# Modulation rows and bias pieces in a fused two-block kernel: where the pieces stand between the rows

## The chip, the core and the metric

The kernel runs on one core of a Trainium2 chip. PE (TensorE) multiplies, DVE (VectorE) and ACT (ScalarE) work on rows of 128 lanes, POOL (GpSimd) does small elementwise work and issues its own DMAs, SP only issues DMAs. Each engine takes its instructions in program order: one that waits holds up all behind it. The metric is the time of one execution on the device in microseconds; lower is better.

## The reference, cut to what matters

Two transformer blocks run one after the other on 256 tokens of width 1024. What the change touches lies in the second block: its modulation vector and the biases of its 32 experts.

```python
cs = jax.nn.silu(c.astype(jnp.float32))
mod = cs @ w_ada[l] + b_ada[l]                       # 6 x 1024 values
sh_a, sc_a, gt_a, sh_f, sc_f, gt_f = jnp.split(mod, 6, axis=-1)
h = modulate(rms_norm(x, g_mix[l]), sh_a, sc_a)
...
def expert_block(args):
    xb, e = args
    u = xb @ w1[e] + b1[e]
    ...
    return a @ w2[e] + b2[e]
```

The modulation needs only c, and the biases need nothing else, so both can be prepared at any time before the second block uses them.

## The kernel before, in words

**The dense stage.** The first 880 us or so are a list of 128 matrix products (`plan`): `w_in`, `w_br_sb`, `w_gate` with `w_br_df`, `w_out`, the feed-forward products and then those of the second block. SP loads each product's weights in tiles `w` of 1 MB. `feed_halves` splits every half tile into a rounded high part on ACT (line 106) and the rest on DVE (line 107); the two are called `hl`, and PE multiplies with them in three products per tile (lines 213 to 215). The pool of `hl` has three buffers, so at most two halves lie ready while PE works through a third. One half is 24 products of 256 columns.

**Ticks.** `run_w` calls `tick()` after every 12 products. A tick lets side work (generators in `sides`) put its next instructions into the program; a generator's `yield n` asks for its next turn n ticks later. Everything is fixed when the program is built: a tick is a place in the instruction streams, no time.

**The side work `ada`.** It computes `mod` in 48 rows of 128 values. `row(j)` has POOL issue a DMA of 512 KB into one of two buffers `wa` (line 267); one custom DVE instruction multiplies the row with `cs` and sums it (line 280). In the 19th round and the five after it, `ada` also calls `bias_parts` once (lines 994 to 1001): POOL loads a piece of the experts' biases into one of the same two buffers `wa` (there called `b`), does six small conversions on it and writes the result to DRAM as `bias_parts`. A row for which there is no free buffer waits, on POOL's queue, until the piece has been written. The rows pause while `st["hold"]` is set, during the last down products of the first block's feed-forward part. `drain_names` (used by `close_heads`) runs ticks with no product between them until the attention heads are done.

**The expert stage**, the rest of the time, streams 402 MB of expert weights through SP's queue.

Of the kernel before, what the change touches and what calls it, by code (L numbers as in the profile page):

```python
# [34 lines left out]
]  # L35


LAG = dict(rs=2, ad0=1, lam=4, bq=12, el=4, bp=18, r1=52, wo=3, rg=21, ada=7, head=6, ffn=2, n2=3, n2b=6, sb0=4, sb1=6, vt=3, df0=1, df1=4, df2=3, df3=8, df4=4, rt0=6, rt1=6, dl0=2, dl1=4, dl2=11, dl3=1)
LAG["in"] = 4


@with_exitstack
def tile_two_blocks(ctx, tc, A, out, dbg=None):
# [31 lines left out]
    def pair(name, n=S, wide=False):  # L75
        return bigt(name + "h", n, F32R, wide=wide), bigt(name + "l", n, F32R, wide=wide)
# [110 lines left out]
    def side(gen, lag=1):  # L187
        sides.append([state["tick"] + lag, gen])
# [62 lines left out]
    def ada():  # L251

        more = bias_parts()
        cs = tmp.tile([P, D], F32, tag="cs", name="cs", bufs=1)
        nc.gpsimd.dma_start(cs, A["c2"].to_broadcast([P, D]))
        t = tmp.tile([P, D], F32, tag="wa", name="wa", bufs=2)
        yield 3
        act(t, cs, AF.Exp, scale=-1.0)
        nc.gpsimd.tensor_scalar_add(t, t, 1.0)
        yield 3  # L260
        for r in range(0, D, 256):
            nc.vector.reciprocal(t[:, r:r + 256], t[:, r:r + 256])
            yield 1
        nc.gpsimd.tensor_mul(cs, cs, t)
        def row(j):
            t = tmp.tile([P, D], F32, tag="wa", name="wa", bufs=2)
            nc.gpsimd.dma_start(t, A["w_ada_2"][j])
            return t

        rows = [row(0)]  # L270
        for j in range(48):
            if j >= LAG["bp"]:
                next(more, 0)
            if j < 47:
                rows.append(row(j + 1))
            yield LAG["ada"]
            while st.get("hold"):
                yield 2
            t = rows.pop(0)
            nc.vector.tensor_tensor_reduce(out=t, in0=t, in1=cs, scale=1.0, scalar=vec[:, V_BADA + j:V_BADA + j + 1],  # L280
                                           op0=ALU.mult, op1=ALU.add, accum_out=mod[:, j:j + 1])


    lam_init = 0.8 - 0.6 * math.exp(-0.3 * 0)
# [43 lines left out]
    def norm_in():  # L328
# [19 lines left out]
        nc.gpsimd.tensor_add(a[:, 0], a[:, 0], a[:, 1])  # L348
        side(in_factor(a), LAG["in"])
        st["os"] = pair("os")  # L350
        st["od"] = pair("od")

    def in_factor(a):
        ss = att.tile([P, 512], F32, tag="at", name="ss")
        mm(ss[:, :L], ones, a[:, 0], start=True, stop=True)
        rs = rsin
        v, t = small(L, "rs")
        first, rest = rsqrt_steps(rs, ss[:, :L], (v, t), 1.0 / D, eps, EPS)
        first()
        yield LAG["rs"]  # L360
        rest()
        st["rsin"] = rs
        st["rs"] = rs[:, NM:L].unsqueeze(1).to_broadcast([P, 2, S])
        st["late"]()
        side(ada(), LAG["ad0"])
        yield LAG["lam"]
        lam()
        yield 1
# [618 lines left out]
    def bias_parts():  # L987

        nc.gpsimd.dma_start(sel, A["sel"])
        for c in range(6):  # L990
            c_ = slice(c * 512, (c + 1) * 512)
            br = tmp.tile([P, D], F32, tag="wa", name="b", bufs=2)
            b, r = br[:96, 0:512], br[:96, 512:768].bitcast(BF16)
            nc.gpsimd.dma_start(b, A["b12"][:, c_])
            nc.gpsimd.tensor_copy(r, b)
            nc.gpsimd.tensor_sub(b, b, r)
            nc.gpsimd.tensor_copy(r[32:64], b[32:64])
            nc.gpsimd.tensor_copy(r[64:96], b[64:96])
            nc.gpsimd.tensor_sub(b[64:96], b[64:96], r[64:96])
            nc.gpsimd.tensor_copy(r[64:96], b[64:96])  # L1000
            nc.gpsimd.dma_start(bsd.ap()[:, c_], r)
            yield

    def spread(to, cols):
        nc.gpsimd.tensor_mul(to, ident.unsqueeze(1).to_broadcast([P, 4, P]), cols.unsqueeze(2).to_broadcast([P, 4, P]))
# [598 lines left out]
```

## Time and profile before

| | |
|---|---|
| median of 3 runs | 1827.83 us (1824.49 to 1828.0) |
| the profiled execution, whole | 1826.24 us |
| its span in the profile | 1824.0 us |
| PE busy | 1739.4 us, 95% of the span |
| DVE busy | 875.0 us, 48% |
| ACT busy | 484.7 us, 27% |
| POOL busy | 123.9 us, 7% |
| mean DMA rate | 313 GB/s |

The span is the time from the first to the last instruction of the profiled execution; its own time is 2.2 us longer. Shares of busy time are means over two stages that have different limits, so they say little by themselves; the stretches below are what to read.

### The profile page before, as it was taken

How to read it: one execution, taken by the hardware profiler on the slowest of the kernel's cores; microseconds unless marked ns; L12 is line 12 of the kernel's file. 1: busy time of each engine (PE TensorE's matmuls, PEld its weight loads, DVE VectorE, ACT ScalarE, POOL GpSimd, SP SyncE). 2: the span in 40 equal slices, each digit the busy share in tenths (PEclk: the TensorE clock that was granted, in tenths of full speed). 3: DMA queues.
4: the chain of work that ended last, by engine and by line, in shares of the span. 5: the costliest groups of instructions: out<-in, count | busy, mean ns of one | idle time of the engine just before them, and what ended most of it. 6: DMA issues, size and time to landing. Idle time of an engine off the chain costs nothing. (4 is left out here: it accounts for less than half of the span.)

```text
span 1824.0 us, 25881 instructions
## 1 busy us (share of the span) xinstructions
PE 1739.4 (95%) x10942; PEld 1145.8 (63%) x10942; DVE 875.0 (48%) x1330; ACT 484.7 (27%) x754; POOL 123.9 (7%) x132
## 2 busy tenths in 40 slices
PE   8999998789999999999999999999999999999987
PEld 7999998789998999999733333333233323332322
DVE  7767776577778667776422223222222222222223
ACT  4545654244435644455300000000000000000001
POOL 2100004520003000000100000000000000000000
PEclk8999999799999999999999999999999999999999
DMA  6446455468665654566899999999999999999996
GB/s 220 170 167 229 158 193 186 167 209 341 245 216 179 245 179 168 204 223 226 309 416 424 423 425 424 424 422 424 422 425 424 423 424 423 424 423 425 422 425 261
DMA packets 107645, 571.82 MB, mean 313 GB/s; under 512 B 11022, under 2 KB 16070, under 8 KB 59654
## 3 DMA queue, kind: packets, MB, share of 16 engines
q1 hardware_dynamic: 96144, 538.46, 74.1%
q0 software_dynamic: 7904, 28.08, 4.6%
q10 hardware_dynamic: 3478, 3.59, 0.6%
q8 instruction: 87, 1.43, 0.3%
q14 instruction: 32, 0.26, 0.0%
HBM read 568.44 MB, written 4.02 MB: 314 GB/s over the span
## 5 line engine op out<-in xcount | busy, mean ns | idle before, releaser
L1265 PE MATMUL u<-mw,xe 128*64 128x512 f32 x2048 | 476.7, 600 | 18.1 <-DMA mw<-in_w_mlp_dram 17.3
L107 DVE TENSOR_TENSOR hl<-w,hl 128x1024 fp32r<-128x1024 f32 (+1 forms) x256 | 318.3, 1257 | 146.6 <-ACT hl L106 146.1
L1265 PEld LDWEIGHTS u<-mw,xe 128*64 128x64 f32 x2048 | 132.7, 136 | 300.1 <-issue 222.8
L106 ACT ACTIVATE hl<-w 128x1024 fp32r<-128x1024 f32 (+1 forms) x256 | 260.1, 1032 | 125.2 <-PE ps L215 74.7
L1299 PE MATMUL y<-mw,aT 128*64 128x512 f32 x992 | 227.7, 597 | 19.6 <-DMA mw<-in_w_mlp_dram 19.4
L1299 PEld LDWEIGHTS y<-mw,aT 128*64 128x64 f32 x992 | 67.2, 136 | 163.2 <-issue 102.0
L1319 DVE TENSOR_TENSOR macc<-macc,cp 128x512 f32<-128x512 f32 x124 | 79.7, 684 | 184.4 <-PE cp L1316 184.4
L213 PE MATMUL ps<-xnh,hl 128*128 128x256 f32 (+1 forms) x512 | 153.3, 299 | 2.4 <-ACT hl L106 2.4
L215 PE MATMUL ps<-xnh,hl 128*128 128x256 f32 (+1 forms) x512 | 149.2, 291 | 6.2 <-DVE hl L107 6.2
L214 PE MATMUL ps<-xnl,hl 128*128 128x256 f32 (+1 forms) x512 | 148.2, 289 | 0.0
L1285 ACT COPY aT<-ap 128x512 f32<-128x512 f32 x31 | 18.2, 586 | 425.6 <-PE ap L1283 425.6
L213 PE MATMUL ps<-h2h,hl 128*128 128x256 f32 x384 | 110.2, 287 | 0.0
L215 PE MATMUL ps<-h2h,hl 128*128 128x256 f32 x384 | 108.7, 283 | 0.0
L214 PE MATMUL ps<-h2l,hl 128*128 128x256 f32 x384 | 108.6, 283 | 0.0
L213 PEld LDWEIGHTS ps<-xnh,hl 128*128 128x128 f32 x512 | 99.2, 194 | 7.3 <-ACT hl L106 3.8
L215 PEld LDWEIGHTS ps<-xnh,hl 128*128 128x128 f32 x512 | 99.0, 193 | 7.3 <-DVE hl L107 7.3
L213 PE MATMUL ps<-hnh,hl 128*128 128x256 f32 x352 | 100.6, 286 | 0.0
L214 PE MATMUL ps<-hnl,hl 128*128 128x256 f32 x352 | 100.3, 285 | 0.0
L215 PE MATMUL ps<-hnh,hl 128*128 128x256 f32 x352 | 100.2, 285 | 0.0
L214 PEld LDWEIGHTS ps<-xnl,hl 128*128 128x128 f32 x512 | 99.0, 193 | 0.1
L1305 DVE TENSOR_TENSOR ys<-y,m 128x512 f32<-128x512 f32 x31 | 21.4, 692 | 138.4 <-PE y L1303 138.4
L1293 DVE COPY m<-gq 128x256 f32<-128x256 f32 x31 | 13.2, 425 | 144.1 <-PE gq L1291 144.1
(466 smaller groups left out, 2934.6 us busy)
## 6 DMA issues: line engine op xcount, KB each, us to landing
mw<-in_w_mlp_dram SPq DMA_DIRECT2D x383, 1024.0 KB, 19.7
w<-in_w_in_dram SPq DMA_DIRECT2D x60, 1024.0 KB, 4.9
wa<-in_w_ada_dram POOLq DMA_DIRECT2D x48, 512.0 KB, 4.8
w<-in_w_ffn_gate_dram SPq DMA_DIRECT2D x11, 1024.0 KB, 5.0
w<-in_w_ffn_up_dram SPq DMA_DIRECT2D x11, 1024.0 KB, 4.8
w<-in_w_gate_dram SPq DMA_DIRECT2D x8, 1024.0 KB, 5.4
w<-in_w_ffn_down_dram SPq DMA_DIRECT2D x8, 1024.0 KB, 5.4
w<-in_w_br_sb_dram SPq DMA_DIRECT2D x4, 1024.0 KB, 6.0
```

Of the source, the lines that this page charges most:

```text
L106: act(hi, src, AF.Copy)
L107: (eng or nc.vector).tensor_sub(lo, src, hi.bitcast(F32))
L213: mm(ps[m], hi[:, k, cs], xh[:, k0 + k, r], start=first, stop=False, skip_group_check=True)
L214: mm(ps[m], hi[:, k, cs], xl[:, k0 + k, r], start=False, stop=False, skip_group_check=True)
L215: mm(ps[m], lo[:, k, cs], xh[:, k0 + k, r], start=False, stop=last, skip_group_check=True)
L1265: mm(u[64 * hf:64 * hf + 64, c * 512:(c + 1) * 512], xk, wcol(hf, c), start=k == 0, stop=False)
L1285: nc.scalar.copy(aT, ap)
L1293: nc.vector.tensor_copy(gT, gq[:, :256])
L1299: mm(y[64 * hf:64 * hf + 64, :], a, wcol(hf), start=k == 0, stop=False)
L1305: nc.vector.tensor_mul(ys, y, gtf)
L1319: nc.vector.tensor_add(d, d, cp[hf])
```

## The change

The first two rows are asked for ahead of the loop. In each round the DVE instruction of the row now comes first; then, in six rounds, a piece of the biases, after which the generator rests for `LAG["bq"]`, 12 ticks; then the row after the next is asked for. The rest ahead of each DVE instruction is 6 ticks where it was 7. `bias_parts` yields `None` so that the loop can tell a piece from the end.

```diff
-LAG = dict(... bq=12, el=4, bp=18, ... ada=7, ...)
+LAG = dict(... bq=12, el=4, bp=18, ... ada=6, ...)
...
-        rows = [row(0)]
+        rows = [row(0), row(1)]
         for j in range(48):
-            if j >= LAG["bp"]:
-                next(more, 0)
-            if j < 47:
-                rows.append(row(j + 1))
             yield LAG["ada"]
             while st.get("hold"):
                 yield 2
             t = rows.pop(0)
             nc.vector.tensor_tensor_reduce(out=t, in0=t, in1=cs, ...)
+
+            if j >= LAG["bp"] and next(more, 1) is None:
+                yield LAG["bq"]
+            if j < 46:
+                rows.append(row(j + 2))
...
             nc.gpsimd.dma_start(bsd.ap()[:, c_], r)
-            yield
+            yield None
```

On every engine the other instructions keep their order; only the row's DVE instruction and POOL's row loads and pieces stand elsewhere between them. Three places follow.

DVE, from the products `w_gate` and `w_br_df` (`gt`, `m1l`) to the first of `w_out` (`xr`, `hnl`), before the change; `wa,mod<-wa,cs,c_vecs` is the instruction of a row:

```order
L107 TENSOR_TENSOR hl<-w,hl 128x1024
L280 ISA wa,mod<-wa,cs,c_vecs 128x1024
L280 ISA mod 128x1
L107 TENSOR_TENSOR hl<-w,hl 128x1024
L529 TENSOR_TENSOR gt<-ps,masks 128x512
L107 TENSOR_TENSOR hl<-w,hl 128x1024 x2
L280 ISA wa,mod<-wa,cs,c_vecs 128x1024
L280 ISA mod 128x1
L547 TENSOR_TENSOR gt<-gt,ysb 128x512
L548 TENSOR_TENSOR gt<-gt,ps 128x512
L549 TENSOR_TENSOR gt<-gt 128x512
L107 TENSOR_TENSOR m1l<-gt,m1h 128x512
```

The same place after the change:

```order
L107 TENSOR_TENSOR hl<-w,hl 128x1024 x2
L276 ISA wa,mod<-wa,cs,c_vecs 128x1024
L276 ISA mod 128x1
L530 TENSOR_TENSOR gt<-ps,masks 128x512
L107 TENSOR_TENSOR hl<-w,hl 128x1024 x2
L548 TENSOR_TENSOR gt<-gt,ysb 128x512
L549 TENSOR_TENSOR gt<-gt,ps 128x512
L550 TENSOR_TENSOR gt<-gt 128x512
L107 TENSOR_TENSOR m1l<-gt,m1h 128x512
L107 TENSOR_TENSOR hl<-w,hl 128x1024 x2
L582 TENSOR_TENSOR xr<-ps,xr 128x2x256
```

Before, a row comes after every three or four splits `hl`, in the rounds with a piece as well; now nine splits lie between two rows of such rounds.

POOL, from a piece to the next piece, reads the same before and after (here after, without the conversions between); what differs is which row the load in the middle brings: before it is the row that DVE's next such instruction takes, after it is the one after that.

```order
L1001 CAST b<-b 32x512
L1002 DMA bias_parts<-b 96x512
L267 DMA wa<-in_w_ada_dram 128x1024
L995 DMA b<-in_b_dram 96x512
L996 CAST b<-b 96x512
```

The load of the row moved to 12 ticks behind the piece in the order in which the program is written; on POOL alone that does not show.

DVE at the end of the heads, inside the ticks without products, before the change (`on` and `odl` are the last steps of a head):

```order
L529 TENSOR_TENSOR gt<-ps,masks 128x512
L280 ISA wa,mod<-wa,cs,c_vecs 128x1024
L280 ISA mod 128x1
L504 SCALAR_TENSOR_TENSOR on<-o,gsub,rsd 128x256
L107 TENSOR_TENSOR odl<-on,odh 128x256
L280 ISA wa,mod<-wa,cs,c_vecs 128x1024
L280 ISA mod 128x1
L504 SCALAR_TENSOR_TENSOR on<-o,gsub,rsd 128x256
L107 TENSOR_TENSOR odl<-on,odh 128x256
L107 TENSOR_TENSOR hl<-w,hl 128x1024 x2
```

The same place after the change:

```order
L530 TENSOR_TENSOR gt<-ps,masks 128x512
L276 ISA wa,mod<-wa,cs,c_vecs 128x1024
L276 ISA mod 128x1
L505 SCALAR_TENSOR_TENSOR on<-o,gsub,rsd 128x256
L107 TENSOR_TENSOR odl<-on,odh 128x256
L276 ISA wa,mod<-wa,cs,c_vecs 128x1024
L276 ISA mod 128x1
L276 ISA wa,mod<-wa,cs,c_vecs 128x1024
L276 ISA mod 128x1
L505 SCALAR_TENSOR_TENSOR on<-o,gsub,rsd 128x256
L107 TENSOR_TENSOR odl<-on,odh 128x256
L107 TENSOR_TENSOR hl<-w,hl 128x1024 x2
```

Before, two rows stood here with a head's `on` and `odl` between them; now there are three, the last two side by side, and the first piece of the biases comes behind the third.

## Rows read from the trace of the kernel before

**Rows 1.** The page: span, busy time, and the granted clock in 40 slices.
```profile
span 1824.0 us, 25881 instructions
PE 1739.4 (95%) x10942; PEld 1145.8 (63%) x10942; DVE 875.0 (48%) x1330; ACT 484.7 (27%) x754; POOL 123.9 (7%) x132
...
PE   8999998789999999999999999999999999999987
...
PEclk8999999799999999999999999999999999999999
```

**Rows 2.** Windows: busy us and instructions (x) by engine, clock, DMA share, GB/s.
```profile
core 0: us, PE busy (x) PEld busy (x) DVE busy (x) ACT busy (x) POOL busy (x), PEclk, DMA share, GB/s
100.00:200.00 100.00, 100.00 (x764) 92.99 (x763) 71.81 (x119) 52.84 (x113) 4.27 (x8) 1.00 0.55 193
285.00:383.00 98.00, 73.37 (x518) 71.20 (x517) 61.70 (x68) 36.76 (x50) 48.98 (x50) 0.84 0.49 170
400.00:540.00 140.00, 140.00 (x1169) 140.00 (x1169) 102.25 (x119) 58.13 (x65) 7.43 (x14) 1.00 0.72 271
540.00:600.00 60.00, 55.99 (x432) 54.24 (x431) 49.59 (x77) 32.59 (x50) 16.84 (x10) 0.97 0.53 180
840.00:1824.00 984.00, 934.31 (x4672) 365.95 (x4670) 279.98 (x516) 81.31 (x137) 11.73 (x11) 1.00 0.98 406
```

**Rows 3.** Waits of PE from 250 to 420 us: total, times, longest.
```profile
PE ps L213 <- ACT m1h L106: 10.4, 1, 10.4
PE ps L215 <- DVE hl L107: 7.2, 4, 2.2
PE ss L320 <- DVE nr L316: 6.0, 1, 6.0
```

**Rows 4.** Timeline of DVE: the first, third and last of five row instructions that waited.
```profile
298.01 1.29 DVE L280 CUSTOM_DVE_ANT_0 wa<-wa,cs,c_vecs 128x1024 f32<-128x1024 f32 x1 [5.64 <-DMA wa<-in_w_ada_dram]
...
331.76 1.28 DVE L280 CUSTOM_DVE_ANT_0 wa<-wa,cs,c_vecs 128x1024 f32<-128x1024 f32 x1 [10.13 <-DMA wa<-in_w_ada_dram]
...
364.96 1.28 DVE L280 CUSTOM_DVE_ANT_0 wa<-wa,cs,c_vecs 128x1024 f32<-128x1024 f32 x1 [3.23 <-DMA wa<-in_w_ada_dram]
```

**Rows 5.** Waits of DVE from 250 to 420 us: the longest group.
```profile
DVE wa L280 <- DMA wa<-in_w_ada_dram: 25.5, 5, 10.1
```

**Rows 6.** Timeline of POOL: one piece and the rows around it.
```profile
291.66 0.53 POOL L994 DMA_DIRECT2D b<-in_b_dram  x1 [0.31 <-issue]
...
306.42 0.52 POOL L1001 DMA_DIRECT2D bias_parts<-b  x1 [0.30 <-POOL b L1000]
308.65 0.58 POOL L267 DMA_DIRECT2D wa<-in_w_ada_dram  x1 [1.71 <-DMA bias_parts<-b]
```

**Rows 7.** The tile wa, whole span: time of its row loads from issue to landing.
```profile
DMA to landing us min/median/max: 3.7/4.8/9.4
```

**Rows 8.** Timeline of DVE at the end of the heads.
```profile
251.12 1.27 DVE L280 CUSTOM_DVE_ANT_0 wa<-wa,cs,c_vecs 128x1024 f32<-128x1024 f32 x1
...
254.86 1.28 DVE L280 CUSTOM_DVE_ANT_0 wa<-wa,cs,c_vecs 128x1024 f32<-128x1024 f32 x1
...
258.53 2.36 DVE L107 TENSOR_TENSOR hl<-w,hl 128x1024 fp32r<-128x1024 f32 x2 [0.53 <-ACT hl L106]
```

**Rows 9.** Timeline of PE there: the first product of `w_br_df` after the heads.
```profile
255.27 0.47 PE L213 MATMUL ps<-odh,hl 128*128 128x256 f32 x1
```

**Rows 10.** Lines of DVE, 285 to 383 us: the splits (busy, mean ns, idle before).
```profile
L107 DVE TENSOR_TENSOR hl<-w,hl 128x1024 fp32r<-128x1024 f32 x22 | 32.0, 1473 | 3.5 <-ACT hl L106 3.3
```

**Rows 11.** The same, 383 to 481 us.
```profile
L107 DVE TENSOR_TENSOR hl<-w,hl 128x1024 fp32r<-128x1024 f32 x35 | 42.0, 1222 | 18.9 <-ACT hl L106 18.9
```

**Rows 12.** Timeline of DVE: the step that the norm's sum waits for.
```profile
370.42 1.64 DVE L316 TENSOR_TENSOR nr<-nr,sq 128x512 f32<-128x512 f32 x1
```

**Rows 13.** Waits of PE from 540 to 600 us.
```profile
PE ps L215 <- DVE hl L107: 3.6, 5, 1.3
PE ps L213 <- ACT hl L106: 0.4, 1, 0.4
```

More of the change, by code (lines that the diff above doesn't have):

```diff
@@ L35 @@
 ]
-LAG = dict(rs=2, ad0=1, lam=4, bq=12, el=4, bp=18, r1=52, wo=3, rg=21, ada=7, head=6, ffn=2, n2=3, n2b=6, sb0=4, sb1=6, vt=3, df0=1, df1=4, df2=3, df3=8, df4=4, rt0=6, rt1=6, dl0=2, dl1=4, dl2=11, dl3=1)
+LAG = dict(rs=2, ad0=1, lam=4, bq=12, el=4, bp=18, r1=52, wo=3, rg=21, ada=6, head=6, ffn=2, n2=3, n2b=6, sb0=4, sb1=6, vt=3, df0=1, df1=4, df2=3, df3=8, df4=4, rt0=6, rt1=6, dl0=2, dl1=4, dl2=11, dl3=1)
 LAG["in"] = 4
```

## The prediction, made blind

> **What bounds the kernel now.** I read the page first [rows 1]: PE is busy 95% of the span, and in the 40 slices it falls to 7 tenths only once inside the dense stage, in the eighth slice (319 to 365 us), where its clock falls too. Then the windows [rows 2]. From 840 us on the DMA share is 0.98 at 406 GB/s: that stage is bound by its weights, and whatever ends the dense stage earlier or later moves it as a whole, because no load of expert weights is moved by the change. In the dense stage two healthy stretches, 100 to 200 and 400 to 540 us, show PE busy all the time. The stretch 285 to 383 us does not: 518 products in 98 us, where 400 to 540 us has 1169 in 140 us, or 8.35 per us. At that rate 518 products take 518 / 8.35 = 62.0 us. So **36.0 us** of PE are lost there, as idle time and as time at a lower clock (mean granted clock 0.84, a mixture of 2.4 and 1.2 GHz).
>
> Who is waited for? PE's waits name DVE's splits, the norm's `nr`, and an `m1h` on ACT that itself follows from DVE's `gt` [rows 3]. DVE's own longest group of waits is the row instruction waiting for its row's DMA, 25.5 us in 5 times [rows 5]. The five stand 16.7 us apart on the mean (298.01 to 364.96 in four steps, [rows 4]), although only 7 ticks, 84 products or 84 / 8.35 = 10.1 us, lie between two of them. POOL shows why [rows 6]: a piece of biases is issued at 291.66, its result is sent at 306.42, and only when that has landed does the row's load go out, at 308.65. That is 17.0 us from piece to row, then 4.8 us median for the row to land [rows 7]. DVE takes its queue in order, so behind the waiting row stand the splits, and PE runs out of them: it has two halves in hand, 48 products or 5.7 us, and the longest wait is 10.13 us.
>
> **The change, part by part.**
>
> *The row is asked for later but used much later.* In the rounds with a piece the row that follows it is loaded 12 ticks after the piece was put into the program, and used 6 + 12 + 6 = 24 ticks after its load was. 12 ticks are 144 products, 17.2 us, about the 17.0 us that the piece takes; 24 ticks are 34.5 us, against a landing of at most 9.4 us. If POOL is some us late with the piece, some 20 us of cover remain; without it each late row would cost what it costs now, about 36.0 / 5 = 7 us. So all five waits should go. Value: the whole 36.0 us as the upper bound; none as the lower one. I start from the upper, since in the stretch from 400 to 540 us, with a row every 10 us and no piece, PE loses nothing.
>
> *What comes back in the same place.* Four terms, each bounded by a row.
>
> First, the end of the heads. Three rows now fall into ticks without products, the last two side by side. The earlier pair stood at 251.12 and 254.86 [rows 8]. The new first one takes the place of 251.12 and ends at 252.4; the load for the third is issued then and lands 3.7 to 9.4 us later, at 256.1 to 261.8, median 257.2; the second ends near 256.2. So the third waits 0 to 5.6 us, median 1.0, and adds 1.28 us of work, ahead of the two splits that started at 258.53. PE starts `w_br_df` at 255.27 [rows 9] with two halves in hand, so it needs the next one at 261.0, and the first of the two splits, 1.2 us long, would end at 258.53 + 1.0 + 1.28 + 1.2 = 262.0: 1.0 us late at the median landing, more beyond it. I take 1.5 us, bounds 0 and 6. Behind that row stand the last head's `on` and `odl` and these splits.
>
> Second, the `w_out` products while POOL works on a piece. POOL slows DVE: splits take 1473 ns in the bad stretch and 1222 ns in the next [rows 10, 11]. The pieces and their work stay, so this stays. A row now stands just ahead of the last join before `w_out`, and its piece runs through the first two of the four products. The nearest case is 540 to 600 us, where POOL works beside similar steps and PE waits 3.6 + 0.4 = 4.0 us [rows 13]; in 400 to 540 us it waits for nothing. I take the middle, 2.0, bounds 0 and 6 (half as much again, for the join).
>
> Third, the norm's sum behind `w_out`: PE waits 6.0 us for `nr` [rows 3], of which 3.23 us are the late row [rows 4]; 2.8 remain, part of them POOL's work beside DVE's (the last step, `nr`, took 1.64 us [rows 12]). A row stands there still, but its piece only begins to load then. I take 2.0, bounds 1 and 3.
>
> Fourth, the clock. Some idle time of PE will remain, and it may fall to 1.2 GHz once or twice; in 540 to 600 us, with 4.0 us of waits, the mean was 0.97, that is 0.03 x 60 = 1.8 us. I take 1.5, bounds 0 and 4.
>
> The SBUF — State Buffer page of the Trainium skill, section "Who interferes with whom", states a stricter rule for the second term: a DVE instruction with two SBUF inputs and a GpSimd instruction that reads SBUF exclude each other for the whole instruction. By it the two splits' excess is no mild slowing, and a DVE step could wait out one POOL step whole. The means of [rows 10, 11] differ by only 0.25 us, so here the collisions are few or short; by the rule at its worst the second term would be its upper bound, and the sum below 25.0 instead of 29.0.
>
> *Rows every 6 ticks instead of 7* outside the six rounds. 84 products become 72, so a row's 1.28 us comes every 8.6 us instead of 10.1: DVE's share rises by 0.15 - 0.127 = 2 points on 72% (100 to 200 us) or 73% (400 to 540 us). A load has two rests, 12 ticks or 17 us, to land in, against 9.4 at most. Cost nothing, hidden under DVE's free quarter; if that cover were gone it is 1.28 us a row. Fewer rows are done when the pause begins, so more follow it, at the end of the first block and in the second; DVE has room there as well, and nothing needs the late columns before `w_o`. Cost nothing.
>
> **Sum.** 36.0 - 1.5 - 2.0 - 2.0 - 1.5 = 29.0 us gained. The profiled execution took 1826.24 us (span 1824.0), 1.6 us under the median of the runs shown: 1826.24 - 29.0 = **1797.2**, I say 1797.
>
> **The rivals.**
>
> *A: contention becomes the bound.* The pieces are spread over 6 x 18 ticks, 155 us, and reach into `w_out`, the norm and the first feed-forward products, where a DVE step late by 2 us is not caught up. For it: POOL busy 49 of 98 us, splits 20% longer. Against it: POOL's total work is the same and thinner. The Trainium skill's SBUF — State Buffer page, in the section named above, states the rule that would make this case. Price: all terms at their upper bounds, 6 + 6 + 3 + 4 = 19, gain 17, so 1809; with half of that more in the feed-forward part (9 us) 1818. Chance 0.12.
>
> *B: the change doesn't do what it says.* POOL's queue holds the same order of pieces and rows as before, and if each row still came out of it too late, the row instruction would wait as now. For it: 17.0 against 17.2 us, no margin at that one point. Against: the row is not needed for another 12 ticks. Result 1826, within 0.2%. Chance 0.04.
>
> *C: the denser rows bind DVE, and the kernel gets slower.* If a row's 1.28 us showed on PE in each of the 42 rounds without a piece, that is 54 us against the 36.0 gained: 1844. It decides from 29 of the 42 on (36.0 / 1.28 is 28). Against: today's rows, at 7 ticks, cost PE no wait at all in 400 to 540 us. Chance 0.03.
>
> **How the numbers follow.** The forecast has 0.81, A 0.12, B 0.04, C 0.03. Its own bounds run from 36.0 - 1 = 35 us gained to 17, so 1791 to 1809; the runs shown scatter by 1.8 us to either side of the profiled one, so I put the range at 1789 to 1807: it takes in the forecast but for its last 2 us, and leaves out B, C and most of A, together some 0.18. The measurement of this kernel tells about 0.2% (3.7 us) from no change; by that line A still counts as faster, so faster 0.93, same 0.04, slower 0.03.
>
> **What would show it.** Right: in the stretch from the heads' end to the feed-forward part the row instruction has no wait for its DMA, or one of 1 to 2 us at the heads' end; the waits of PE for `m1h` (10.4) and `nr` (6.0) shrink to about 0 and 2; the windows there hold 8 products per us at a clock near 1.0; the expert stage lasts as long as before and starts 29 us earlier. Wrong: waits of DVE for `wa` elsewhere, splits well over 1473 ns around `w_out`, or waits of PE for `hl` spread over 60 to 250 or 400 to 640 us.

## The result, and the profile after

The changed kernel takes 1798.72 us (median of 4 runs, 1797.16 to 1801.05); the kernel before took 1827.91 us beside it (1824.49 to 1828.0). The ratio on record is 0.9852, with a 95% interval of 0.9839 to 0.9865 (the two medians alone would give 0.9840). The forecast was 1797, range 1789 to 1807. The profiled execution has a span of 1794.9 us, 29.1 us less than the 1824.0 of [rows 1].

The page of the changed kernel shows the granted clock at nine tenths or more in every slice, the one that had dipped among them:

```profile
span 1794.9 us, 25881 instructions
...
PE 1729.0 (96%) x10942; PEld 1135.6 (63%) x10942; DVE 871.2 (49%) x1330; ACT 483.7 (27%) x754; POOL 120.5 (7%) x132
...
PEclk9999999999999999999999999999999999999999
```

The windows of the changed kernel (busy us and instructions by engine, clock, DMA share, GB/s) answer to [rows 2]. The stretch in which PE had lost 36.0 us of 98 now runs at 533 products in 67 us, 8.0 per us, where the healthy stretch of before had 8.35:

```profile
core 0: us, PE busy (x) PEld busy (x) DVE busy (x) ACT busy (x) POOL busy (x), PEclk, DMA share, GB/s
250.00:285.00 35.00, 32.32 (x250) 30.27 (x250) 25.11 (x31) 19.14 (x32) 9.49 (x12) 1.00 0.59 203
285.00:352.00 67.00, 64.61 (x533) 63.90 (x532) 51.80 (x61) 35.81 (x49) 24.66 (x27) 1.00 0.54 188
```

PE's waits in the changed kernel from 250 to 400 us (total, times, longest) answer to [rows 3]. The 10.4 us for `m1h` are gone, the norm's wait fell from 6.0 to 1.4 us:

```profile
PE ps L215 <- DVE hl L107: 2.5, 3, 1.6
PE ss L321 <- DVE nr L317: 1.4, 1, 1.4
PE ps L213 <- ACT hl L106: 0.5, 1, 0.5
PE o L500 <- ACT sq L498: 0.5, 1, 0.5
...
```

DVE's wait for a row's DMA, 25.5 us in 5 times in [rows 5], is one wait of 0.3 us, and it stands at the end of the heads. Its timeline there answers to [rows 8]; the row instruction is at line 276 now:

```profile
251.22 1.28 DVE L276 CUSTOM_DVE_ANT_0 wa<-wa,cs,c_vecs 128x1024 f32<-128x1024 f32 x1
...
254.88 1.28 DVE L276 CUSTOM_DVE_ANT_0 wa<-wa,cs,c_vecs 128x1024 f32<-128x1024 f32 x1
...
256.50 1.28 DVE L276 CUSTOM_DVE_ANT_0 wa<-wa,cs,c_vecs 128x1024 f32<-128x1024 f32 x1 [0.33 <-DMA wa<-in_w_ada_dram]
...
259.62 2.36 DVE L107 TENSOR_TENSOR hl<-w,hl 128x1024 fp32r<-128x1024 f32 x2 [0.52 <-ACT hl L106]
```

POOL's timeline of one piece answers to [rows 6]. This piece takes 303.31 - 287.48 = 15.8 us up to the row behind it (the six take 12.2 to 15.8 us, those of the kernel before 14.6 to 18.0); what is new is that POOL then sits idle for 7.07 us, until DVE has freed the next buffer. POOL is no longer the engine that sets the pace:

```profile
287.48 0.53 POOL L995 DMA_DIRECT2D b<-in_b_dram  x1 [13.96 <-DVE mod L276]
...
298.51 0.52 POOL L1002 DMA_DIRECT2D bias_parts<-b  x1 [0.30 <-POOL b L1001]
303.31 0.58 POOL L267 DMA_DIRECT2D wa<-in_w_ada_dram  x1 [4.28 <-DMA bias_parts<-b]
310.95 0.53 POOL L995 DMA_DIRECT2D b<-in_b_dram  x1 [7.07 <-DVE mod L276]
```

So the waits that the forecast named are gone. Which of the three edits does it was not separated by the forecast, and that is what the experiments ask: the order (a row asked for before the piece), the rest (12 ticks behind a piece), and the step (6 ticks for 7).

### The profile page after: what moved, and what is told of

It is laid out like the page before. It is cut to its first block, busy times and chain, and to the rows that moved or that the text cites. A ratio compares the mean times of both kernels' runs of the same rounds, so it can differ in the third digit from the quotient of the medians.

```text
span 1794.9 us, 25881 instructions
## 1 busy us (share of the span) xinstructions
PE 1729.0 (96%) x10942; PEld 1135.6 (63%) x10942; DVE 871.2 (49%) x1330; ACT 483.7 (27%) x754; POOL 120.5 (7%) x132
```

## The experiments

Two theories stand against each other. The period: POOL needs some 17 us for a piece and the row load behind it, and a round that is shorter than that runs late, in whatever order its parts stand. The order: what counts is that a row is asked for one round ahead of its use. Times are medians; the kernel before ran at 1824 to 1826 us beside them, and ratios to it are what to compare.

**The order without the rest.** The changed kernel, with

```diff
-            if j >= LAG["bp"] and next(more, 1) is None:
-                yield LAG["bq"]
+            if j >= LAG["bp"]:
+                next(more, 1)
```

> The changed kernel without the rest of 12 ticks after a piece: row instruction, piece, load of the row after the next, 6 ticks. Theory (the period: a round with a piece can't be shorter than the 17.0 us that POOL takes for piece and row load, whatever stands first): six rounds of 6 ticks are 51.6 us against 6 x 17.0 = 102 us of POOL; the last late row lands 6 us after that, so the rows fall back by up to 48 us, less the 5.7 us of splits that PE has in hand: some 40 us slower than the changed kernel, 1832 to 1842, slower than the kernel before, with five or six waits of the row instruction for its DMA. Rival (the order: asking a row ahead of the piece is what helps): 1797 to 1801, no such waits.

Measured: 1826.03 us, ratio 1.0004 (0.9994 to 1.0014). The whole gain is gone. DVE waits for rows again, 22.7 us in 6 times. The row loads behind the pieces, from 270.97 to 342.45 us, are six, 14.3 us apart, and between them POOL never waits for DVE. These are the wait of DVE, then the second and the third load:

```profile
DVE wa L276 <- DMA wa<-in_w_ada_dram: 22.7, 6, 7.8
```

```profile
286.85 0.57 POOL L267 DMA_DIRECT2D wa<-in_w_ada_dram  x1
288.95 0.53 POOL L995 DMA_DIRECT2D b<-in_b_dram  x1 [1.53 <-DMA bias_parts<-b]
291.86 1.69 POOL L996 CAST b<-b 96x512 bf16<-96x512 f32 x1 [2.38 <-DMA b<-in_b_dram]
...
300.25 0.53 POOL L1002 DMA_DIRECT2D bias_parts<-b  x1 [0.31 <-POOL b L1001]
300.77 0.57 POOL L267 DMA_DIRECT2D wa<-in_w_ada_dram  x1
```

The order theory falls here. The size was below the expected range (1832 to 1842), because a round of POOL is shorter than the 17.0 us on which it was worked out. Here, from the second round on, the row's load goes out right behind the store; it is the next piece's load that waits until the store has landed, while the row is under way, and its first conversion starts 2.9 us after its issue. In the kernel before the row's load waits for the store, the piece's load goes out only behind the row's, and its first conversion starts 6.7 us after its issue (291.66 in [rows 6]):

```profile
298.38 1.38 POOL L995 CAST b<-b 96x512 bf16<-96x512 f32 x1 [6.19 <-DMA b<-in_b_dram]
```

Two rows ahead are not the reason: the kernel before with steps of 6 (below) asks for one row ahead and its row loads do not wait for the store either, while with a rest of 2 there are two ahead and they wait. What decides between the two patterns is not shown. With the measured round: 6 x (14.3 - 8.6) = 34 us, less the 5.7 us that PE has in hand, is 28; measured against the changed kernel's 1798.72 are 27. The sum is a rough estimate, made after the result: for the kernel before it gives 6 x (17.0 - 10.1) - 5.7 = 36 us, where 29 were measured.

**The rest without the order.** The kernel before, with

```diff
-            if j >= LAG["bp"]:
-                next(more, 0)
+            if j >= LAG["bp"] and next(more, 1) is None:
+                yield LAG["bq"]
```

> The kernel before with the rest alone: piece, 12 ticks, load of the next row, 7 ticks, row instruction; one row under way ahead, steps of 7. Theory (the period): a round now has 19 ticks, 27.3 us, against 17.0 us for the piece and up to 7.2 us for the row to land, 24.2 us: no wait, 1797 to 1802. Rival (the order): the row still comes out of POOL's queue directly behind its piece, so the waits stay: 1820 to 1828.

Measured: 1797.19 us, ratio 0.9847 (0.9826 to 0.9867). The whole gain is there with one row asked for only behind its piece; DVE has no wait for a row from 250 to 450 us. DVE's row instructions show rounds of 24 to 32 us with room in them: the row is asked for at 287.49 and taken at 301.25.

```profile
287.49 0.57 POOL L267 DMA_DIRECT2D wa<-in_w_ada_dram  x1 [1.98 <-DMA bias_parts<-b]
302.83 0.53 POOL L994 DMA_DIRECT2D b<-in_b_dram  x1 [14.77 <-DVE mod L280]
```

```profile
270.70 1.28 DVE L280 CUSTOM_DVE_ANT_0 wa<-wa,cs,c_vecs 128x1024 f32<-128x1024 f32 x1
...
301.25 1.28 DVE L280 CUSTOM_DVE_ANT_0 wa<-wa,cs,c_vecs 128x1024 f32<-128x1024 f32 x1
```

**Steps of 7.** The changed kernel with `ada=7`.

> The changed kernel with steps of 7 ticks again. Theory (the step costs and gives nothing, since DVE has a free quarter): 1797 to 1801, the same as the changed kernel. Rival (denser rows cost PE at the heads' end or take from DVE): 3 us or more faster or slower than 1798.7.

Measured: 1795.75 us, ratio 0.9836 (0.9816 to 0.9857). Below the theory's range, and 3 us under the 1798.7 from which the rival counts its 3 us: undecided by this run alone, and run again below.

**The pieces elsewhere.** The changed kernel with `bp=29` in place of 18, so that all six pieces fall into the feed-forward products.

> The changed kernel with the first piece in the 30th round (29 for 18), so that all six fall into the feed-forward products and not beside the end of the heads, w_out and the norm. Theory (what is left of the lost time, 36.0 - 29 = 7 us, is DVE slowed by the pieces where it has little to spare): the waits of PE from 250 to 360 us, some 5 us, go, and 1793 to 1796. Rival (they come from those places themselves, or move with the pieces): 1797 to 1801.

Measured: 1799.12 us, ratio 0.9861 (0.9841 to 0.9881). Not faster. At the old place the norm still costs 1.9 us (`ss` on `nr`) with no piece near it. From the heads' end to `w_out` the kernel is 2.5 us faster than the changed one (65.2 and 67.7 us, see below), but from there to the expert stage it is 2.7 us slower (550.1 and 547.4 us), and PE has a wait of 0.7 us for a split from 360 to 520 us, where the changed kernel has none. So the idea that the rest of the lost time is bound to that place is half right: part of the cost moves with the pieces.

**A rest of 6.** The changed kernel with `bq=6`.

> The changed kernel with a rest of 6 ticks instead of 12: a round with a piece is 12 ticks, 17.2 us. In the run without the rest POOL took some 14 us from piece to piece. Theory (the period of a round against POOL's): 17.2 is more than 14, no wait for a row worth more than 1 to 2 us, 1796 to 1801. Rival (the pieces' work beside DVE's costs more the closer they stand): 1803 or more.

Measured: 1803.57 us, ratio 0.988 (0.9864 to 0.9897). No row is waited for beyond 0.5 us, so the period holds; but the kernel lies some 5 us above the changed one, outside the expected 1796 to 1801, and inside what the rival said. Against the second measurement of the changed kernel (1799.99, below) it is 3.6 us, and the intervals of the ratios meet, so the size is not settled. That denser pieces cost is what the splits suggest: from 255 to 345 us a split takes 1420 ns on the mean here and 1310 ns in the changed kernel, and 1222 ns where POOL is quiet [rows 11]. These are the lines of DVE in that stretch, first of this run, then of the changed kernel:

```profile
L107 DVE TENSOR_TENSOR hl<-w,hl 128x1024 fp32r<-128x1024 f32 x28 | 39.1, 1420 | 10.4 <-ACT hl L106 10.2
```

```profile
L107 DVE TENSOR_TENSOR hl<-w,hl 128x1024 fp32r<-128x1024 f32 x29 | 37.4, 1310 | 12.1 <-ACT hl L106 12.0
```

**A rest of 2.** The changed kernel with `bq=2`.

> The changed kernel with a rest of 2 ticks: a round is 8 ticks, 11.5 us, some 2.5 us less than POOL's 14. Theory (the period): six rounds fall back by 15 us, less up to 5.7 us that PE has in hand, plus some time at the low clock: 1805 to 1815, between the run without a rest and the one with 6. Rival (any rest will do, since the row is asked for ahead): 1797 to 1801.

Measured: 1822.62 us, ratio 0.9991 (0.9981 to 1.0). Far above the expected 1805 to 1815. The size was wrong because the 14 us of the run without a rest were carried over: here the row's load waits for the store again (1.71 to 4.08 us), and POOL's rounds are 17.0 us (row loads at 271.47 and 356.41 us, five rounds apart). With that, 6 x (17.0 - 11.5) - 5.7 = 27 us; measured against the changed kernel are 24. The waits are back as well, 17.8 us in 5 times.

```profile
271.47 0.57 POOL L267 DMA_DIRECT2D wa<-in_w_ada_dram  x1 [2.18 <-DMA bias_parts<-b]
...
288.17 0.57 POOL L267 DMA_DIRECT2D wa<-in_w_ada_dram  x1 [1.71 <-DMA bias_parts<-b]
...
306.51 0.57 POOL L267 DMA_DIRECT2D wa<-in_w_ada_dram  x1 [4.08 <-DMA bias_parts<-b]
```

**Lighter pieces in both kernels.** Five of a piece's six conversions are left out, and with them the low parts of the biases:

```diff
             nc.gpsimd.tensor_copy(r, b)
-            nc.gpsimd.tensor_sub(b, b, r)
-            nc.gpsimd.tensor_copy(r[32:64], b[32:64])
-            nc.gpsimd.tensor_copy(r[64:96], b[64:96])
-            nc.gpsimd.tensor_sub(b[64:96], b[64:96], r[64:96])
-            nc.gpsimd.tensor_copy(r[64:96], b[64:96])
```

> The kernel before, with pieces that keep their load, one conversion and the store but leave out the other five conversions, so the low parts of the biases are lost. A piece with its row then takes some 10 to 11 us of POOL instead of 17.0, against 10.1 us for 7 ticks. Theory (the period): the waits for rows go nearly, 1798 to 1808. Rival (the order, one row asked for only behind its piece): the row still lands 5 to 7 us after the piece and is waited for each time, 1815 to 1825.

Measured: 1795.01 us, ratio 0.9839 (0.9823 to 0.9856). The kernel before, with its order, its steps and no rest, loses its waits as soon as a piece fits into a round: DVE waits for a row once, 2.2 us. Row loads stand 11.1 us apart (282.94 to 338.63 in five rounds), against the 10.1 us of 7 ticks. It came out below the expected 1798 to 1808, since the 1 us by which a round is too long adds up, over six rounds, to about the 5.7 us that PE has in hand. This is one round of POOL:

```profile
296.00 0.55 POOL L267 DMA_DIRECT2D wa<-in_w_ada_dram  x1 [4.53 <-DMA bias_parts<-b]
296.54 0.52 POOL L994 DMA_DIRECT2D b<-in_b_dram  x1
302.92 1.10 POOL L995 CAST b<-b 96x512 bf16<-96x512 f32 x1 [5.86 <-DMA b<-in_b_dram]
304.31 0.52 POOL L996 DMA_DIRECT2D bias_parts<-b  x1 [0.30 <-POOL b L995]
307.32 0.56 POOL L267 DMA_DIRECT2D wa<-in_w_ada_dram  x1 [2.49 <-DMA bias_parts<-b]
```

> The changed kernel with the same lightened pieces (five of six conversions left out, the low parts of the biases lost). Theory (what is left of PE's waits around the heads' end and the norm comes from those places, not from POOL beside DVE): at most 2 us faster, 1795 to 1800. Rival (POOL slows DVE there): 4 us or more faster, 1793 and below.

Measured: 1794.77 us, ratio 0.9833 (0.9817 to 0.985). The two kernels are now the same within their intervals, which says once more that order and rest only matter through the piece's length. By the medians it is some 4 us faster than the changed kernel, between the two expectations; the intervals of the ratios (0.9839 to 0.9865 there) overlap, so that POOL beside DVE costs a few us in the changed kernel is likely and not settled to the microsecond.

**Once more, side by side.** First the step alone (the kernel before with `ada=6`), then the changed kernel and two neighbours.

> The kernel before with steps of 6 ticks instead of 7 and nothing else. Theory (the period): six rounds of 6 ticks fall behind POOL's 17.0 us by 8.4 us each where those of 7 ticks fell behind by 6.9, so some 7 to 9 us slower than before, 1832 to 1838. Rival (the rows cost what they cost whenever they come): the same as before, within 3 us.

Measured: 1828.47 us, ratio 1.0015 (1.0006 to 1.0025): slower, by 2 to 3 us where 7 to 9 were expected. DVE waits 32.1 us in 7 times. The direction is the period's. The size was worked out with rounds of 17.0 us, and here they are 14.2 us (row loads at 268.39 and 339.58, five rounds apart), because the row's load does not wait for the store and the piece's load does, as in the run without a rest. With that, 6 x (14.2 - 8.6) - 5.7 = 28 us; measured against the changed kernel beside it (1799.99) are 28.

```profile
268.39 0.57 POOL L267 DMA_DIRECT2D wa<-in_w_ada_dram  x1
270.74 0.53 POOL L994 DMA_DIRECT2D b<-in_b_dram  x1 [1.77 <-DMA bias_parts<-b]
...
339.58 0.58 POOL L267 DMA_DIRECT2D wa<-in_w_ada_dram  x1 [0.25 <-issue]
```

> The changed kernel once more, in one call with its neighbours: 1795 to 1800, the mark for the two that follow.

Measured: 1799.99 us (1797.98 to 1802.73), ratio 0.9861 (0.9846 to 0.9876).

> The changed kernel with steps of 7, in the same call. Theory (the step gives nothing): within 2 us of the changed kernel. Rival (steps of 7 are better): 2 us or more faster.

Measured: 1795.37 us (1794.54 to 1798.93), ratio 0.9838 (0.9825 to 0.9852).

> The kernel before with the rest alone, in the same call. Theory (the order gives nothing): within 2 us of the changed kernel with steps of 7, whose only difference is the order. Rival (the order is worth something of its own): 2 us or more slower than that.

Measured: 1796.67 us (1794.3 to 1797.72), ratio 0.9842 (0.9828 to 0.9855).

The order is worth nothing that can be measured (steps of 7 with it: 0.9838, without: 0.9842). Steps of 7 are 4.6 us better than steps of 6 by the medians, as the rival said, and were also ahead in their first run. Most of it can be seen between the first product of `w_br_df` behind the heads and the first step behind `w_out` (PE's `ps<-odh`, DVE's `xr`), in the timelines of the changed kernel and of the one with steps of 7:

```profile
255.29 0.47 PE L213 MATMUL ps<-odh,hl 128*128 128x256 f32 x1
...
269.69 0.39 PE L215 MATMUL ps<-xnh,hl 128*128 128x256 f32 x1 [1.58 <-DVE hl L107]
```

```profile
322.96 0.68 DVE L582 TENSOR_TENSOR xr<-ps,xr 128x512 f32<-128x512 f32 x1
```

```profile
254.40 0.47 PE L213 MATMUL ps<-odh,hl 128*128 128x256 f32 x1
```

```profile
319.27 0.68 DVE L582 TENSOR_TENSOR xr<-ps,xr 128x512 f32<-128x512 f32 x1
```

That is 67.7 against 64.9 us from the same start to the same step; PE idles for 2.4 and 0.7 us of it. With steps of 6 the 19th round, and with it the first piece, falls into the end of the heads: POOL's conversions start at 263.47 us, just where the splits, the join and the third row crowd DVE, and PE waits 1.6 us for a split at 269.69. With steps of 7 the first piece comes later (its load is issued at 284.78 us, where it was 258.09). The changed kernel's second run takes 68.4 us for the stretch, though its longest wait for a split there is 0.9 us; the two runs with steps of 6 whose pieces were moved or lightened take 65.2 and 64.2 us. So in this stretch it is the first piece at that place and not the density of the rows. The stretch explains 2.8 of the 4.6 us; the rest is not located.

## Why the prediction was right, step by step

**The loss and who is waited for.** 36.0 us of PE were put down to late rows, and 29.1 us came back (spans 1824.0 and 1794.9). The first product of the expert stage begins 28.8 us earlier (899.1 and 870.3 us), and what follows it takes as long as before (924.9 and 924.6 us), so the whole gain passed on, as forecast.

**"The row is asked for later but used much later."** The five waits went, as this step said. Its reason was too wide: it counted 24 ticks from load to use, which is what order and rest give together. The experiments show that the rest by itself is enough, that the order by itself gives nothing, and that a shorter piece does the same with neither. What decides is whether a round is longer than POOL's piece with its row load, 17.0 us on the mean in the kernel before. Rival B's bare margin (17.0 against 17.2 us) was therefore the right thing to look at: with 8 ticks, 11.5 us, most of the loss is back (24 of 29 us).

**What comes back in the same place.** 36.0 - 29.1 = 6.9 us were left, where the four terms had 7.0. That the sum fits to 0.1 us is luck: singly the terms are less good. End of the heads (1.5): the third row waited 0.3 us in place of 1.0, but the first piece's work beside DVE, which this term left out, made PE wait for splits there (1.6 us) and stretched the part up to `w_out` by about 3 us. `w_out` (2.0): besides that one, PE's other waits for splits from 250 to 400 us add up to 0.9 us. The norm (2.0): 1.4 us; it stayed at 1.9 and 1.4 us with the pieces moved or lightened, so POOL's part in it, which the term named, is not seen. The clock (1.5): nothing, the granted clock is 1.00 through the stretch. What the terms and the waits leave open, some 2 us, has no line of its own.

**POOL beside DVE.** Rival A's mechanism is likely real, but small: 4 to 5 us by medians with a rest of 6, some 4 us when pieces are lightened, both at the edge of the intervals. The Trainium skill's SBUF — State Buffer page, section "Who interferes with whom", says that a DVE instruction with two SBUF inputs and a GpSimd instruction that reads SBUF keep each other out for the whole instruction. A step of the join in the changed kernel bears this out in kind: `gt` (line 550) took 1.56 us at 264.32 us beside POOL's subtraction, and 0.69 us on the mean in the kernel with steps of 7, where POOL was quiet. The subtraction ran on for 1.0 us behind the step's start, and the step took 0.87 us longer.

```profile
264.32 1.56 DVE L550 TENSOR_TENSOR gt<-gt 128x512 f32<-128x512 f32 x1
```

```profile
264.17 1.16 POOL L997 TENSOR_TENSOR b<-b 96x512 f32<-96x512 f32 x1
```

```profile
L550 DVE TENSOR_TENSOR gt<-gt 128x512 f32<-128x512 f32 x2 | 1.4, 691 | 0.1
```

**"Rows every 6 ticks cost nothing."** Missed by some 3 to 5 us by medians, of which 2.8 us come through the shift of the first piece. Rival C (DVE bound by rows) is out: the kernel got faster, and outside the stretch PE's waits hardly changed (from 400 to 860 us 4.6 us in the changed kernel, from 420 to 860 us 4.0 us before).

**A better version.** The rest with steps of 7, in either order of row and piece (1795.37 and 1796.67 us), beats both kernels by its medians; against the changed kernel (1799.99) the runs barely touch and the intervals of the ratios overlap slightly.

## What to carry to other kernels

When several pieces of side work share one in-order queue, compare the length of a round in the program with the length of the queue's work in a round before looking at how far ahead a load is asked for: here asking earlier did not remove the lateness, while a longer round or a shorter piece did. A wait on an engine off the critical path becomes the critical one when instructions behind it in its queue feed the bound engine with only two buffers of slack. The length of a queue's round is itself no constant: read it in each variant, since here it was 14 or 17 us depending on which load waited for the store. When such work is spread out, look also at what it lands on, since a change of step by one tick moved the first piece onto a crowded spot of DVE's and cost some 3 us there.

## What was not expected of the hardware

Two POOL conversions of the same form and size, 32x512 elements, took 0.60 and 1.59 us in a single piece of the changed kernel (293.13 and 296.62 us), so a piece's length is no constant of its instructions. From its load to the row's load a piece took 14.6 to 18.0 us in the kernel before and 12.2 to 15.8 us in the changed one. The rounds without a pause were 17.0 us on the mean where the row's load waited for the store and 14.2 to 14.3 us where the piece's load did.

```profile
293.13 0.60 POOL L998 CAST b<-b 32x512 bf16<-32x512 f32 x1
...
296.62 1.59 POOL L1001 CAST b<-b 32x512 bf16<-32x512 f32 x1
```
